# A two-layer hybrid transformer in one kernel: four steps of lead at the ends of a phase, later transposes, paired attention scores

## The chip, the cores and the metric

The kernel runs on one core of one Trainium2 chip. The metric is the device time of one execution in microseconds. Within a core five engines work side by side, each on its own queue in order: PE (matrix multiply; its weight loads are listed apart, as PEld), DVE (vector), ACT (scalar functions), POOL, and SP, which here only issues DMAs.

## The reference

Two layers on 256 tokens of width 1024, everything in float32. A layer adds to the residual `x` a feed-forward block, a mixer and a second feed-forward block:

```python
x = x + 0.5 * swiglu(rms_norm(x, ffa_norm), ffa_w_in, ffa_w_out)     # 1024 -> 2*2816 -> 1024
h = rms_norm(x, mix_norm)
(c_q, c_kv, k_rope, g_q, g_k, g_v, g_b, g_a, g_z, m_qkv, gate_logits) = split(h @ w_in)
o_mla  = causal softmax attention, 8 heads, q and k of 96 made from c_q, c_kv and k_rope
o_gdn  = gated delta rule, 4 heads of 128, after a causal convolution over 4 tokens
o_moba = causal softmax attention, 8 heads of 64 (256 tokens are one block)
x = x + sum_n(sigmoid(gate_n) * (o_n @ w_branch_n)) @ w_out
x = x + 0.5 * swiglu(rms_norm(x, ffb_norm), ffb_w_in, ffb_w_out)
```

The delta rule needs the inverse of a unit lower triangular matrix for each head and chunk.

## The kernel before

**Weights.** A weight matrix is read in pieces of 128 x 1024 numbers (a Step). `fetch` (L238) issues the DMA of a piece into one of five `raw` buffers, and splits it in two halves, each by an ACT cast to the rounded part `wh` (L260) and a DVE subtraction for the rest `wl` (L261). There are seven `wh`/`wl` pairs (NW). A product is three matmuls: high by high, high by low, low by high (L280 to L282 with tokens as the stationary operand; L309/L311, L340 to L342 and L965/L966 with the weights as the stationary operand).

**Phases, steps and events.** Each layer has three phases: feed-forward, mixer, feed-forward. A plain step is used twice, once for each half of the tokens: t=0 (the first 128) and t=1. `phase` (L1185) lists these uses, the events: t=0 of a step runs SKEW = 3 steps ahead of t=1 throughout the phase, so a phase begins with three t=0 events and ends with three t=1 events. A joint step (both halves of the tokens at once) is used at its t=1 place. Each event has 6 to 12 matmuls, and after it `fetch` splits at most one more half, up to LEAD = 3 steps past the last t=0 step.

**Generators and ticks.** What follows a product (norms, transposes, softmax, the delta rule) is written as Python generators. `tick` (L133) runs after each event and resumes those that are due; `yield n` means n ticks later. `until` runs ticks without events until something that is needed has been emitted.

**The planner.** Outside the first few instructions the framework orders each engine's instructions by itself: of those that its own estimates hold ready, the one emitted first. So a `yield` moves the place of an instruction in that order and promises nothing.

**Three chains that end in transposes on PE.** `epi_first` (L466): ACT copies a product of the first feed-forward step (L471), one tick later PE transposes it (L476). `epi_kv` (L1027): keys of the first attention, the last DVE product is L1041, one tick later `qk_T` transposes (L997). `epi_m(1)` (L1087): keys of the third branch; POOL makes 1/norm (L364, L365), DVE multiplies (L1108), one tick later `qk_T` transposes (L997).

**Phase ends.** `residual` (L428) adds the last product to `x`, squares it on ACT, POOL takes the power -1/2 (L392), DVE scales (L396), and LAG = 2 ticks later PE transposes the result (L370) for the next phase. This happens for t=0 and three events later for t=1.

**Attention** (`attention`, L560; used for both softmax branches). A written list says in which order groups of heads get their scores (`s0`: the first 128 queries of four heads; `s1`: the other 128 of two heads) and pairs of heads their outputs (`o`). `scores` holds one of two PSUM banks (`hold`, L118), does the score matmuls of its heads one after the other (L574), adds the mask (L576), takes the maximum on DVE (L581), one tick later the exponentials on ACT (L586, bank free after that), one tick later the division (L592). `outputs` transposes (L604 to L606), copies on ACT (L608) and, a tick later, does two matmuls for each of two heads (L613, L614), the two heads on different column halves of the array. Entries of the list are Y_ATT = 3 ticks apart. In the first branch the heads have 96 rows; in the third they have 64, even heads on partitions 0 to 63 and odd heads on 64 to 127, and each `s0` or `s1` group there has heads of one parity only. Every float32 matmul here is two MATMUL instructions.

**Inverse** (`invert` in `gdn`, L739). For two levels, a product of 128 columns for each of 4 heads (L772), an ACT copy (L774), a second product of 128 columns (L780), and a DVE addition that takes only every second group of columns (L783). A `back` transpose (L669) begins each level; the first waits for a DMA that brings the diagonal blocks' inverses.

**Where a branch waits.** The first `w_branch` step of a branch calls `until` on that branch's output.

Of the kernel before, what the change touches and what calls it, by code (L numbers as in the profile page):

```python
# [12 lines left out]
OP = mybir.AluOpType  # L13
# [20 lines left out]

LEAD, SKEW = 3, 3
NB4, NB2, NRAW, NW = 15, 20, 5, 7
# [45 lines left out]
class Kern:  # L82
# [34 lines left out]

    def hold(self):  # L118

        while self.held["pm"] >= BANKS - 4:  # L120
            yield 1
        self.held["pm"] += 1

# [325 lines left out]
    def ffn(self, l, name, norm_after):  # L449
# [16 lines left out]
        def epi_first(t, ps):  # L466

            if t == 0:
                SG["first"] = self.b4().rearrange("p (k c) -> p k c", k=4)
            y = self.b2()  # L470
            nc.scalar.copy(y, ps)  # L471
            self.done("acc")
            yield 1
            p = self.tp()
            for k in range(4):
                nc.tensor.transpose(p[:, k * 128:(k + 1) * 128], y[:, k * 128:(k + 1) * 128], self.ident)  # L476
            g = SG["first"]
# [82 lines left out]
    def attention(self, plan, getq, getk, getv, rq, oT):  # L560
# [7 lines left out]

        def scores(hs, n, w, q0, dst):
            t = q0 // 128  # L570
            yield from self.hold()
            ps = self.pm().rearrange("p (h k) -> p h k", h=n)
            for i, h in enumerate(hs):
                mm(ps[:, i, :], getq(h)[:, q0:q0 + 128], getk(h)[:, 0:w], start=(i == 0), stop=False,  # L574
                   skip_group_check=True)
            mm(ps[:, :, w - 128:w], self.identb, self.maskA[:, None, :].to_broadcast([128, n, 128]), start=False, stop=True,  # L576
               skip_group_check=True)
            dh = hs[1] - hs[0]
            rqs = rq[t][:, hs[0]:hs[-1] + 1:dh]
            mx, nb, sm, rs = (self.sm(4)[:, 0:n] for _ in range(4))  # L580
            nc.vector.tensor_reduce(mx, ps, axis=AX.X, op=OP.max)  # L581
            nc.vector.scalar_tensor_tensor(nb, mx, -1.0, rqs, op0=OP.mult, op1=OP.mult)
            yield 1
            P = self.b2().rearrange("p (h k) -> p h k", h=n)
            for h in range(n):
                nc.scalar.activation(P[:, h, :], ps[:, h, :], AF.Exp, scale=rqs[:, h:h + 1], bias=nb[:, h:h + 1],  # L586
                                     accum_out=sm[:, h:h + 1])
            self.done("pm")
            yield 1
            nc.vector.reciprocal(rs, sm)  # L590
            for h in range(n):
                nc.scalar.activation(P[:, h, :], P[:, h, :], AF.Copy, scale=rs[:, h:h + 1])  # L592
            for i, h in enumerate(hs):
                dst[h] = P[:, i, :]
            left[0] -= 1

        def outputs(hs):
            while not all(h in P0 and h in P1 for h in hs):
                yield 1
            yield 1  # L600
            PT = []
            for h in hs:
                pt = self.tp().rearrange("p (j k) -> p j k", j=4)
                nc.tensor.transpose(pt[:, 0, :], P0[h], self.ident)  # L604
                nc.tensor.transpose(pt[:, 1, :], P1[h][:, 0:128], self.ident)
                nc.tensor.transpose(pt[:, 2, :], P1[h][:, 128:256], self.ident)  # L606
# [4 lines left out]
            for i, h in enumerate(hs):  # L611
# [7 lines left out]
        for what, hs in plan:  # L619
            if what == "o":  # L620
                yield from outputs(hs)
            else:
# [5 lines left out]
    def gdn(self, ready, sil, beta, g, zs, oT):  # L628
# [110 lines left out]
        def invert(c):  # L739
# [29 lines left out]
            for l in range(LEVELS - 1):  # L769
                p = v4(self.pm())  # L770
                for h in range(H):
                    mm(p[:, h, :], cm[:, h, :], zz[:, h, 0, :], start=True, stop=True)  # L772
                t1 = v4(self.b2())
                nc.scalar.copy(t1, p)  # L774
                cm = v4(self.b2())
                nc.gpsimd.tensor_tensor(cm, nk, brow(self.lev[l + 1]), op=OP.mult)
                yield Y_INV
                p = v4(self.pm())
                for h in range(H):
                    mm(p[:, h, :], zz[:, h, 1, :], t1[:, h, :], start=True, stop=True)  # L780
                even = lambda z: z.rearrange("p h (m s b) -> p h m s b", s=2, b=16 << l)[:, :, :, 0, :]
                v = even(zz[:, :, 0, :])
                nc.vector.tensor_tensor(v, even(p), v, op=OP.add)  # L783
                yield Y_INV
# [97 lines left out]
    def mixer(self, l, norm_after):  # L882
# [144 lines left out]
        def epi_kv(t, hg, ps):  # L1027
            p = ps.rearrange("p (h d) -> p h d", h=4)
            if ("av", t) not in d:
# [12 lines left out]
                                    rk[:, :, None].to_broadcast([128, 4, 32]), op=OP.mult)  # L1042
            yield 1
            qk_T(t, y, 96, ("akT", hg))
# [15 lines left out]
        def attend():  # L1060
# [11 lines left out]
            while not all(("turned", ("mT", i), 1) in d for i in range(2)) or ("mv", 1) not in d:  # L1072
# [14 lines left out]
        def epi_m(i):  # L1087
            def f(t, ps):
# [16 lines left out]
                else:  # L1105
                    self.rsq(r, r, EPS, 1.0 / 64)
                    yield 2
                    nc.vector.tensor_tensor(y, y, r[:, :, None].to_broadcast([128, 8, 64]), op=OP.mult)  # L1108
                    yield 1
                qk_T(t, y.rearrange("p (k j) d -> p k (j d)", j=2), 128, ("mT", i))  # L1110
# [72 lines left out]


    def phase(self, steps, nacc):  # L1185

        n = len(steps)
        self.nacc = nacc
        ev = [(0, i) for i in range(SKEW)]
        for i in range(SKEW, n):  # L1190
            ev += [(1, i - SKEW), (0, i)]
        ev += [(1, i) for i in range(n - SKEW, n)]
        for t, i in ev:
# [4 lines left out]
            if t == 0:  # L1198
# [3 lines left out]
                if s.before:  # L1202
                    s.before()
            self.fetch(self.splits < 2 * (self.head + 1 + LEAD))
            if s.joint:
                for _ in s.use(s.wh, s.wl):
                    self.tick()
                    self.fetch(self.splits < 2 * (self.head + 1 + LEAD))
            else:
                s.use(t, s.wh, s.wl)  # L1210
            self.tick()
            if t == 1:
                s.wh = s.wl = s.raw = None
        self.base += n

    def run(self):
        self.setup()
        self.ss = {}
        self.base = self.loaded = self.splits = self.head = 0
        gains = [(n, l) for l in range(L) for n in ("ffa_norm", "mix_norm", "ffb_norm")]  # L1220
# [77 lines left out]
```

## Time and profile before

| what | value |
|---|---|
| three runs | 1353.65, 1350.1, 1348.01 us; median 1350.1 us |
| the profiled execution's own time | 1350.52 us |
| its span, first to last instruction | 1348.5 us |
| PE busy | 1320.3 us, 98% of the span |
| DVE, ACT, POOL busy | 937.4, 786.9, 117.9 us (70%, 58%, 9%) |
| granted PE clock, mean | 1.000 |
| HBM | 227.11 MB read, 170 GB/s over the span |

Busy time of PE is the time in which at least one matmul is under way, from its start to its modelled end; neighbouring matmuls overlap, so the distance from one start to the next is what a matmul costs in a full stream. An idle time stands in square brackets with the instruction that ended it.

### The profile page before, as it was taken

Reading aid. Unit: us, or ns where it says so; the run is one execution under the profiler, and the core shown is the slowest. Engines: PE = TensorE matmul, PEld = TensorE weight load, DVE = VectorE, ACT = ScalarE, POOL = GpSimd, SP = SyncE. Lnnn points to the kernel's source line nnn. Section 1 sums busy time; section 2 is a strip of 40 time slices with the busy share of each in tenths; the row PEclk is TensorE's granted clock in tenths of the full one; section 3 lists DMA queues with packets and bytes.
Section 4 is the critical chain, followed back from the end, with each engine's and each line's share of the span. In section 5 each row is a group of like instructions: output and inputs, shape, how many; then the busy total and the mean of one; then the engine's idle time right before and its main releaser. Section 6 shows DMA issues by size and latency. Waiting matters only on the chain.

```text
span 1348.5 us, 21398 instructions
## 1 busy us (share of the span) xinstructions
PE 1320.3 (98%) x7786; PEld 1150.3 (85%) x7786; DVE 937.4 (70%) x1890; ACT 786.9 (58%) x1783; POOL 117.9 (9%) x157
## 2 busy tenths in 40 slices
PE   6999999999999999999999999999999999999998
PEld 5888888788999988888888888887889999888887
DVE  6777558888457677775577775588865576777752
ACT  6666447776654556664466654487656544666642
POOL 0010003711101000000000000044120000000000
PEclk9999999999999999999999999999999999999999
DMA  8765566566343657665666556555553445666551
GB/s 277 233 221 185 177 181 167 145 169 176 103 131 110 188 156 218 188 189 176 197 196 194 185 176 184 158 173 160 153 157 99 139 127 171 187 188 189 191 184 62
DMA packets 207561, 231.25 MB, mean 171 GB/s; under 512 B 15616, under 2 KB 166112, under 8 KB 207456
## 3 DMA queue, kind: packets, MB, share of 16 engines
q1 hardware_dynamic: 207456, 229.89, 56.4%
q8 instruction: 61, 1.00, 0.3%
q14 instruction: 44, 0.36, 0.1%
HBM read 227.11 MB, written 2.75 MB: 170 GB/s over the span
## 4 chain that ended last, share of the span: by engine, by line
PE 92%; DVE 3%; ACT 2%; POOL 1%; DMA 1%; issue 1%; SPq 0%; DVEq 0%; ACTq 0%; POOLq 0%
PE acc L309 22%; PE acc L311 11%; PE acc L280 10%; PE acc L282 10%; PE acc L281 10%; PE acc L340 5%; PE acc L341 5%; PE acc L342 5%; PE acc L965 3%; PE pm L574 2%; PE acc L966 1%; ACT wh L260 1%; DMA raw<-in_ffa_w_in 1%; DVE wl L261 1%; PE tp L370 1%; PE pm L613 1%
## 5 line engine op out<-in xcount | busy, mean ns | idle before, releaser
L261 DVE TENSOR_TENSOR wl<-raw,wh 128x512 fp32r<-128x512 f32 (+1 forms) x844 | 563.2, 687 | 265.7 <-ACT wh L260 265.4
L260 ACT CAST wh<-raw 128x512 fp32r<-128x512 f32 (+1 forms) x844 | 497.2, 619 | 389.7 <-issue 147.4
L309 PE MATMUL acc<-q,wh 128*128 128x512 f32 x1280 | 449.3, 396 | 0.0
L311 PE MATMUL acc<-q,wl 128*128 128x256 f32 x1280 | 359.2, 281 | 0.0
L309 PEld LDWEIGHTS acc<-q,wh 128*128 128x128 f32 x1280 | 240.1, 188 | 55.8
L280 PE MATMUL acc<-wh,q 128*128 128x512 f32 (+2 forms) x656 | 259.1, 395 | 1.4 <-ACT q L358 1.4
L282 PE MATMUL acc<-wh,q 128*128 128x512 f32 (+2 forms) x656 | 256.1, 390 | 0.0
L281 PE MATMUL acc<-wl,q 128*128 128x512 f32 (+2 forms) x656 | 255.5, 390 | 0.0
L311 PEld LDWEIGHTS acc<-q,wl 128*128 128x128 f32 x1280 | 242.4, 189 | 0.5
L340 PE MATMUL acc<-q,wh 128*128 128x256 f32 x576 | 168.3, 292 | 0.0
L341 PE MATMUL acc<-q,wh 128*128 128x256 f32 x576 | 163.2, 283 | 0.4 <-DVE q L359 0.4
L342 PE MATMUL acc<-q,wl 128*128 128x256 f32 x576 | 163.0, 283 | 0.0
L280 PEld LDWEIGHTS acc<-wh,q 128*128 128x128 f32 x656 | 123.9, 189 | 26.3 <-ACT q L358 2.4
L282 PEld LDWEIGHTS acc<-wh,q 128*128 128x128 f32 x656 | 123.5, 188 | 26.2 <-DVE q L359 2.2
L281 PEld LDWEIGHTS acc<-wl,q 128*128 128x128 f32 x656 | 123.8, 189 | 21.7
L340 PEld LDWEIGHTS acc<-q,wh 128*128 128x128 f32 x576 | 110.3, 192 | 1.8 <-issue 1.0
L341 PEld LDWEIGHTS acc<-q,wh 128*128 128x128 f32 x576 | 110.3, 191 | 1.2 <-DVE q L359 0.8
L342 PEld LDWEIGHTS acc<-q,wl 128*128 128x128 f32 x576 | 110.1, 191 | 0.1
L965 PE MATMUL acc<-q,wh 128*128 128x512 f32 x192 | 70.5, 406 | 0.0
L486 DVE TENSOR_TENSOR d<-d,acc 128x256 f32<-128x256 f32 x160 | 66.5, 416 | 5.3 <-ACT d L484 5.3
L484 ACT COPY d<-acc 128x256 f32<-128x256 f32 x160 | 58.8, 368 | 18.9 <-PE acc L311 18.8
L392 POOL TENSOR_TENSOR s<-s,mhalf 128x1 f32<-128x1 f32 x12 | 8.3, 691 | 634.3 <-DVE s L385 634.3
(203 smaller groups left out, 1280.9 us busy)
## 6 DMA issues: line engine op xcount, KB each, us to landing
raw<-in_w_in SPq DMA_DIRECT2D x104, 512.0 KB
raw<-in_ffa_w_in SPq DMA_DIRECT2D x88, 512.0 KB
raw<-in_ffb_w_in SPq DMA_DIRECT2D x88, 512.0 KB
raw<-in_ffa_w_out SPq DMA_DIRECT2D x44, 512.0 KB
raw<-in_ffb_w_out SPq DMA_DIRECT2D x44, 512.0 KB
raw<-in_w_branch SPq DMA_DIRECT2D x24, 512.0 KB
raw<-in_w_out SPq DMA_DIRECT2D x16, 512.0 KB
raw<-in_w_in SPq DMA_DIRECT2D x8, 416.0 KB
```

Of the source, the lines that this page charges most:

```text
L260: nc.scalar.copy(s.wh[:, v], s.raw[:, v])
L261: nc.vector.tensor_sub(s.wl[:, v], s.raw[:, v], s.wh[:, v].bitcast(F32))
L280: mm(o, xh, wh[:, j, :], start=(k == 0), stop=False)
L281: mm(o, xh, wl[:, j, :], start=False, stop=False)
L282: mm(o, xl, wh[:, j, :], start=False, stop=(k == nk - 1))
L309: mm(ps.rearrange("p (s c) -> p s c", s=2), wh[:, k, v], x2, start=(g == 0 and k == 0), stop=False, skip_group_check=True)
L311: mm(ps[:, 0:256], wl[:, k, v], x2[:, 0, :], start=False, stop=last, skip_group_check=True)
L340: mm(o, wh[:, k, v], xh, start=(g == 0 and c == 0 and k == 0), stop=False, skip_group_check=True)
L341: mm(o, wh[:, k, v], xl, start=False, stop=False, skip_group_check=True)
L342: mm(o, wl[:, k, v], xh, start=False, stop=(4 * g + k == nk - 1), skip_group_check=True)
L486: nc.vector.tensor_tensor(dst, dst, ps[:, 0:256], op=OP.add)
L965: mm(p, wh[:, k, :], self.X[k // 2][:, k % 2], start=(k == 0), stop=False, skip_group_check=True)
```

## The change

It has five parts, in one diff. (1) t=0 runs four steps ahead (WIDE) at the start and at the end of each phase and three elsewhere; `ahead` keeps the splits within the seven buffers. (2) `epi_first`, `epi_kv` and `epi_m(1)` transpose one tick later. (3) `scores` takes a list of groups, holds as many banks, and issues their matmuls in turn; the list of the third branch now pairs an even group with an odd one (7 entries for 10). (4) `outputs` issues the larger matmuls of both heads, then the smaller ones. (5) the two products of the inverse are done on the 64 columns a head that are used.

```diff
-LEAD, SKEW = 3, 3
+LEAD, SKEW, WIDE = 3, 3, 4
-    def hold(self):
-        while self.held["pm"] >= BANKS - 4:
+    def hold(self, n=1):
+        while self.held["pm"] + n > BANKS - 4:
             yield 1
-        self.held["pm"] += 1
+        self.held["pm"] += n
...
             y = self.b2()                      # epi_first
             nc.scalar.copy(y, ps)
             self.done("acc")
-            yield 1
+            yield 2
...
-        def scores(hs, n, w, q0, dst):
+        def scores(groups, n, w, q0, dst):
...
-            for i, h in enumerate(hs):
-                mm(ps[:, i, :], getq(h)[:, q0:q0 + 128], getk(h)[:, 0:w], start=(i == 0), stop=False,
-                   skip_group_check=True)
-            mm(ps[:, :, w - 128:w], self.identb, self.maskA[:, None, :].to_broadcast([128, n, 128]), start=False, stop=True,
-               skip_group_check=True)
+            yield from self.hold(len(groups))
+            banks = [self.pm().rearrange("p (h k) -> p h k", h=n) for _ in groups]
+            for i in range(n):
+                for hs, ps in zip(groups, banks):
+                    mm(ps[:, i, :], getq(hs[i])[:, q0:q0 + 128], getk(hs[i])[:, 0:w], start=(i == 0), stop=False,
+                       skip_group_check=True)
+            for ps in banks:
+                mm(ps[:, :, w - 128:w], self.identb, self.maskA[:, None, :].to_broadcast([128, n, 128]), start=False,
+                   stop=True, skip_group_check=True)
...
-            for i, h in enumerate(hs):
-                ov = o[64 * i:64 * i + 64, :]
-                mm(ov, getv(0, h), PT[i][:, 0:256], start=True, stop=False, skip_group_check=True)
-                mm(ov[:, 128:256], getv(1, h), PT[i][:, 256:384], start=False, stop=True, skip_group_check=True)
+            halves = [(o[64 * i:64 * i + 64, :], h, PT[i]) for i, h in enumerate(hs)]
+            for ov, h, pt in halves:
+                mm(ov, getv(0, h), pt[:, 0:256], start=True, stop=False, skip_group_check=True)
+            for ov, h, pt in halves:
+                mm(ov[:, 128:256], getv(1, h), pt[:, 256:384], start=False, stop=True, skip_group_check=True)
...
             for l in range(LEVELS - 1):        # invert
-                p = v4(self.pm())
+                even = lambda z: z.rearrange("p h (m s b) -> p h m s b", s=2, b=16 << l)[:, :, :, 0, :]
+                half = lambda z: z[:, 0:256].rearrange("p (h c) -> p h c", h=H)
+                v = even(zz[:, :, 0, :])
+                p = half(self.pm())
                 for h in range(H):
-                    mm(p[:, h, :], cm[:, h, :], zz[:, h, 0, :], start=True, stop=True)
-                t1 = v4(self.b2())
+                    mm(p[:, h, :], cm[:, h, :], v[:, h], start=True, stop=True)
+                t1 = half(self.b2())
...
-                nc.vector.tensor_tensor(v, even(p), v, op=OP.add)
+                nc.vector.tensor_tensor(v, p.rearrange("p h (m b) -> p h m b", b=16 << l), v, op=OP.add)
...
-                [("s0", (0, 2, 4, 6)), ("s0", (1, 3, 5, 7)), ("s1", (0, 2)), ("s1", (1, 3)), ("o", (0, 1)),
-                 ("s1", (4, 6)), ("o", (2, 3)), ("s1", (5, 7)), ("o", (4, 5)), ("o", (6, 7))],
+                [("s0", (0, 2, 4, 6), (1, 3, 5, 7)), ("s1", (0, 2), (1, 3)), ("o", (0, 1)), ("s1", (4, 6), (5, 7)),
+                 ("o", (2, 3)), ("o", (4, 5)), ("o", (6, 7))],
...
+    def ahead(self):
+        return self.splits < 2 * min(self.head + 1 + LEAD, self.tail + NW)
...
-        ev = [(0, i) for i in range(SKEW)]
-        for i in range(SKEW, n):
-            ev += [(1, i - SKEW), (0, i)]
-        ev += [(1, i) for i in range(n - SKEW, n)]
+        ev = [(0, i) for i in range(WIDE)]
+        a, b = WIDE, 0
+        while b < n:
+            ev.append((1, b))
+            b += 1
+            while a < n and a - b < (WIDE if b < 2 or a > n - 4 else SKEW):
+                ev.append((0, a))
+                a += 1
...
-            self.fetch(self.splits < 2 * (self.head + 1 + LEAD))
+            self.fetch(self.ahead())
```

In `epi_kv` and `epi_m(1)` the last `yield 1` ahead of `qk_T` is a `yield 2`, as in `epi_first`; `self.tail` is the number of steps whose t=1 use is done.

## Rows read from the trace of the kernel before

**Rows 1.** The page, part 1: busy us, share of the span and count by engine.
```profile
PE 1320.3 (98%) x7786; PEld 1150.3 (85%) x7786; DVE 937.4 (70%) x1890; ACT 786.9 (58%) x1783; POOL 117.9 (9%) x157
```

**Rows 2.** Waits of PE: total us, times, longest us.
```profile
PE tp L370 <- DVE d L396: 12.0, 8, 9.3
PE tp L669 <- DMA q<-zd: 4.5, 4, 1.4
PE tp L997 <- DVE d L1108: 4.2, 4, 1.4
```

**Rows 3.** Timeline near 255 us: start, duration, engine, line, operation, idle before.
```profile
254.60 0.40 PE L965 MATMUL acc<-q,wh 128*128 128x512 f32 x1
...
255.72 0.63 PE L997 MATMUL tp<-ident,d 128*128 128x128 f32 x4 [0.72 <-DVE d L1108]
```

**Rows 4.** Timeline near 262 us, the same chain for t=1.
```profile
260.94 1.78 POOL L365 TENSOR_TENSOR s<-s,mhalf 128x8 f32<-128x8 f32 x1
...
261.75 0.48 PE L282 MATMUL acc<-wh,q 128*128 128x512 f32 x1
...
262.76 0.73 DVE L1108 TENSOR_TENSOR d<-d,s 128x512 f32<-128x512 f32 x1 [1.53 <-POOL s L365]
...
263.64 0.63 PE L997 MATMUL tp<-ident,d 128*128 128x128 f32 x4 [1.41 <-DVE d L1108]
```

**Rows 5.** Timeline near 29 us, the transposes of epi_first for t=1.
```profile
28.44 0.28 PE L311 MATMUL acc<-q,wl 128*128 128x256 f32 x1
...
28.80 0.28 PE L311 MATMUL acc<-q,wl 128*128 128x256 f32 x1
...
29.51 0.66 PE L476 MATMUL tp<-ident,d 128*128 128x128 f32 x4 [0.44 <-ACT d L471]
```

**Rows 6.** Timeline of PE around one s0 group of the third branch.
```profile
340.22 0.28 PE L342 MATMUL acc<-q,wl 128*128 128x256 f32 x1
340.43 1.16 PE L574 MATMUL pm<-q,q 64*128 64x128 f32 x8
...
341.55 0.47 PE L340 MATMUL acc<-q,wh 128*128 128x256 f32 x1
341.86 0.28 PE L341 MATMUL acc<-q,wh 128*128 128x256 f32 x1
```

**Rows 7.** Timeline of PE around one s1 group of the third branch.
```profile
356.06 0.28 PE L342 MATMUL acc<-q,wl 128*128 128x256 f32 x1
356.27 1.13 PE L574 MATMUL pm<-q,q 64*128 64x256 f32 x4
...
357.37 0.36 PE L340 MATMUL acc<-q,wh 128*128 128x256 f32 x1
357.57 0.28 PE L341 MATMUL acc<-q,wh 128*128 128x256 f32 x1
```

**Rows 8.** Timeline of PE in two output groups, of 291 and 303 us.
```profile
291.08 0.66 PE L613 MATMUL pm<-d,d 128*64 128x256 f32 x4
291.56 0.40 PE L614 MATMUL pm<-d,d 128*64 128x128 f32 x4
...
303.08 0.81 PE L613 MATMUL pm<-d,d 128*64 128x256 f32 x3
...
303.94 0.38 PE L614 MATMUL pm<-d,d 128*64 128x128 f32 x2
```

**Rows 9.** Timeline of PE: one column against 128, both with 128-column weights.
```profile
319.15 1.59 PE L683 MATMUL tp<-cst,q 128*128 128x1 f32 x13
...
338.02 1.05 PE L772 MATMUL pm<-q,d 128*128 128x128 f32 x8
```

**Rows 10.** Costliest groups by line (count, busy us, mean ns): ACT's softmax.
```profile
L586 ACT ACTIVATE d<-pm,s,s 128x128 f32<-128x128 f32 (+1 forms) x64 | 32.0, 508 | 18.9 <-DVE s L582 18.9
...
L592 ACT ACTIVATE d<-d,s 128x128 f32<-128x128 f32 (+1 forms) x64 | 25.2, 457 | 1.7 <-DVE s L590 1.6
```

**Rows 11.** Waits of ACT for a weight buffer that PE still reads.
```profile
ACT wh L260 <- PE acc L341: 70.1, 44, 4.1
```

More of the change, by code (lines that the diff above doesn't have):

```diff
@@ L567, in attention @@
         left = [len(plan)]
-        def scores(hs, n, w, q0, dst):
+        def scores(groups, n, w, q0, dst):
             t = q0 // 128
-            yield from self.hold()
-            ps = self.pm().rearrange("p (h k) -> p h k", h=n)
-            for i, h in enumerate(hs):
-                mm(ps[:, i, :], getq(h)[:, q0:q0 + 128], getk(h)[:, 0:w], start=(i == 0), stop=False,
-                   skip_group_check=True)
-            mm(ps[:, :, w - 128:w], self.identb, self.maskA[:, None, :].to_broadcast([128, n, 128]), start=False, stop=True,
-               skip_group_check=True)
[L578 to L582, printed above, removed]
-            yield 1
[L584 to L588, printed above, removed]
-            yield 1
-            nc.vector.reciprocal(rs, sm)
-            for h in range(n):
-                nc.scalar.activation(P[:, h, :], P[:, h, :], AF.Copy, scale=rs[:, h:h + 1])
-            for i, h in enumerate(hs):
-                dst[h] = P[:, i, :]
@@ new lines, in scores @@
+            made = []
+            for hs, ps in zip(groups, banks):
+                rqs = rq[t][:, hs[0]:hs[-1] + 1:hs[1] - hs[0]]
+                mx, nb = (self.sm(4)[:, 0:n] for _ in range(2))
+                nc.vector.tensor_reduce(mx, ps, axis=AX.X, op=OP.max)
+                nc.vector.scalar_tensor_tensor(nb, mx, -1.0, rqs, op0=OP.mult, op1=OP.mult)
+                made.append((hs, ps, rqs, nb))
+            yield 1
+            soft = []
+            for hs, ps, rqs, nb in made:
+                P, sm = self.b2().rearrange("p (h k) -> p h k", h=n), self.sm(4)[:, 0:n]
+                for h in range(n):
+                    nc.scalar.activation(P[:, h, :], ps[:, h, :], AF.Exp, scale=rqs[:, h:h + 1], bias=nb[:, h:h + 1],
+                                         accum_out=sm[:, h:h + 1])
+                self.done("pm")
+                soft.append((hs, P, sm))
@@ L595, in scores @@
+            yield 1
+            for hs, P, sm in soft:
+                rs = self.sm(4)[:, 0:n]
+                nc.vector.reciprocal(rs, sm)
+                for h in range(n):
+                    nc.scalar.activation(P[:, h, :], P[:, h, :], AF.Copy, scale=rs[:, h:h + 1])
+                for i, h in enumerate(hs):
+                    dst[h] = P[:, i, :]
             left[0] -= 1
@@ L610, in outputs @@
             o = self.pm()[:, 0:256]
-            for i, h in enumerate(hs):
-                ov = o[64 * i:64 * i + 64, :]
-                mm(ov, getv(0, h), PT[i][:, 0:256], start=True, stop=False, skip_group_check=True)
-                mm(ov[:, 128:256], getv(1, h), PT[i][:, 256:384], start=False, stop=True, skip_group_check=True)
+            halves = [(o[64 * i:64 * i + 64, :], h, PT[i]) for i, h in enumerate(hs)]
[3 more added lines that the diff above has]
+                mm(ov[:, 128:256], getv(1, h), pt[:, 256:384], start=False, stop=True, skip_group_check=True)
             k = hs[0] // 2
@@ L617, in outputs @@
             left[0] -= 1
-        for what, hs in plan:
+        for what, *hs in plan:
             if what == "o":
-                yield from outputs(hs)
+                yield from outputs(hs[0])
             else:
@@ L777, in invert @@
                 yield Y_INV
-                p = v4(self.pm())
+                p = half(self.pm())
                 for h in range(H):
                     mm(p[:, h, :], zz[:, h, 1, :], t1[:, h, :], start=True, stop=True)
-                even = lambda z: z.rearrange("p h (m s b) -> p h m s b", s=2, b=16 << l)[:, :, :, 0, :]
-                v = even(zz[:, :, 0, :])
-                nc.vector.tensor_tensor(v, even(p), v, op=OP.add)
+                nc.vector.tensor_tensor(v, p.rearrange("p h (m b) -> p h m b", b=16 << l), v, op=OP.add)
                 yield Y_INV
@@ L1042, in epi_kv @@
                                     rk[:, :, None].to_broadcast([128, 4, 32]), op=OP.mult)
-            yield 1
+            yield 2
             qk_T(t, y, 96, ("akT", hg))
@@ L1108, in f @@
                     nc.vector.tensor_tensor(y, y, r[:, :, None].to_broadcast([128, 8, 64]), op=OP.mult)
-                    yield 1
+                    yield 2
                 qk_T(t, y.rearrange("p (k j) d -> p k (j d)", j=2), 128, ("mT", i))
@@ L1207, in phase @@
                     self.tick()
-                    self.fetch(self.splits < 2 * (self.head + 1 + LEAD))
+                    self.fetch(self.ahead())
             else:
@@ L1213, in phase @@
                 s.wh = s.wl = s.raw = None
+                self.tail = g + 1
         self.base += n
@@ L1218, in run @@
         self.ss = {}
-        self.base = self.loaded = self.splits = self.head = 0
+        self.base = self.loaded = self.splits = self.head = self.tail = 0
         gains = [(n, l) for l in range(L) for n in ("ffa_norm", "mix_norm", "ffb_norm")]
```

## The prediction

> **What bounds the kernel now.** I read the page first: PE is busy for 1320.3 of 1348.5 us, and no other engine is above 70% [rows 1]. So PE is the bound, and the change can win in two ways only: where PE idles (28.2 us by that row), or where its matmuls take longer than they must. Busy time hides the second. I therefore read PE's waits next and then the distances between the starts of neighbouring matmuls, in the timeline. Of the idle time, 12.0 us stand at the transposes after a norm, but 9.3 of them are one wait, the start of the kernel; seven at phase ends share 2.7. The other two large ones are 4.5 us for the DMA ahead of the inverse and 4.2 us at L997 for DVE's L1108 [rows 2].
>
> **The later transposes (part 2).** Before L997 a 512-column matmul starts at 254.60 and the transposes only at 255.72 [rows 3]; such a matmul takes 0.24 of a stream (the pair of 512 and 256 columns takes 28.80 - 28.44 = 0.36, its larger part two thirds) [rows 5], so 0.88 is lost. For t=1 it is 263.64 - 261.75 - 0.24 = 1.65; there L1108 itself came late, because POOL's power of 1.78 us ended just before it [rows 4]. Both waits are for L1108, and recur in layer two: four times, 4.2 us by the waits view [rows 2], 2 x (0.88 + 1.65) = 5.06 by the starts. One tick more puts one event between: four pairs of 0.36 [rows 5], 1.44 us. That covers 0.88 whole and leaves 0.21 of the 1.65: gain 2 x (0.88 + 1.44) = 4.6. L1108 itself isn't moved, so nothing on DVE or POOL changes. Bounds: 0, if the planner puts the transposes where they were, and 5.06. In `epi_first` the transposes start 0.71 after a 256-column matmul that takes 0.12 [rows 5]: 0.6 gained, once. `epi_kv` had no wait: 0. But its keys are now a tick later, so the first attention starts and ends a tick later, and the first `w_branch` step, which by the code's order already spends two ticks without events waiting for it, spends three. The tick more holds a product of the inverse (eight matmuls of L772) that only changes places with the step behind it: 0; were it a bare wait, it would be one event, 1.44 a layer.
>
> **Scores in turn (part 3).** An s0 group now costs: the matmul before it starts at 340.22 and would be done after 0.12; the next stream starts at 341.55 and its second matmul 0.31 later instead of 0.12: 1.33 - 0.12 + 0.19 = 1.40 [rows 6]. An s1 group: 357.37 - 356.06 - 0.12 + 0.08 = 1.27 [rows 7]. Six groups a layer, two s0 and four s1, become three pairs. In a pair, the even heads sit on partitions 0 to 63 and the odd ones on 64 to 127, so two halves of the array work. No row shows two row halves at work together; the nearest is the output groups, where two heads use the two column halves: four L613 and four L614 take 291.08 to 291.56 + 0.40 = 0.88, tail included, while one head's four alone would stream 2 x 0.24 + 2 x 0.12 = 0.72 [rows 5, 8]. Two heads thus cost hardly more than one. If row halves do the same, the second group of a pair costs only its mask, 0.2 for s0 and 0.1 for s1: 1.40 - 0.2 = 1.2 and 1.27 - 0.1 = 1.17 saved, a layer 1.2 + 2 x 1.17 = 3.5, both layers 7.1. The other end: the halves take turns, and a pair saves only the gaps on either side of a group: 340.43 - 340.22 - 0.12 = 0.09 before, and about the same twice after (first to second matmul, last to mask), 0.28 x 6 = 1.7. I take 6.5, near the upper end, because the output row is that near.
>
> The Trainium skill, TensorE: Matmul & The Clock Gate, section "Part 3: Packing small matmuls", gives 3.07 times for four row tiles, 77% of the ideal. No run here shows it; as an estimate from that page a pair would stream 0.86 / 0.77 instead of 0.86 and the gain of this part would be 7.1 - 6 x 0.26 = 5.5.
>
> Softmax comes in bursts of two groups. ACT needs (32.0 + 25.2) / 24 groups = 2.4 us a group [rows 10], 4.8 a pair, and two pairs are three ticks apart, 4.3 us: ACT falls behind by one or two us beside its splits. In this stretch the steps are joint, so their halves are split six steps, twelve events, ahead of use: 17 us of cover. I count 0.5 against the change for banks that come free later; between 0 and the rival below.
>
> **Outputs (part 4).** In program order L614 of the first head stands before L613 of the second. In the first group of [rows 8] all four L613 start before any L614, so PE already pulls the second head forward, and the new order gains nothing; only the group of 303 us, where the second head's copy was late, runs 303.08 to 303.94 + 0.38 = 1.24 instead of 0.88. It and its like in layer two: 2 x 0.36 = 0.7 at most, I take 0.6.
>
> The same section of the Trainium skill has matmuls start and end strictly in program order. By that rule sixteen output groups would each have waited as the slow one did, and the reorder would be worth 16 x 0.36 = 5.8. The trace disagrees for the group of 291 us, and the measurement decides.
>
> **The inverse (part 5).** 64 MATMULs each at L772 and L780 go from 128 to 64 columns. But 13 matmuls of one column take 1.59 and 8 of 128 columns 1.05: five more for 0.54, 0.11 each [rows 9], the same price whatever the columns, since both load 128 columns of weights. So 0 on PE. The upper end, half price, is 128 x 0.054 = 6.9. ACT's shorter copies are off the path.
>
> **Four steps ahead (part 1).** The transposes after a norm stay two ticks behind their product, and it is these two events that don't cover the chain; an event between them and the next phase covers what wasn't late. So the 2.7 [rows 2] stays: 0. It may win up to 2.7 where DVE is less crowded. At the kernel's start step 3 is wanted one event earlier, 1.44 at worst.
>
> **Sum.** 4.6 + 0.6 + 6.5 + 0.6 - 0.5 = 11.8 off the profiled execution's own 1350.5 us: 1338.7. The median of the runs, 1350.1, is 0.4 lower: 1338.3, said as 1338.5.
>
> **Rivals.**
> - Row halves take turns: 1.7 instead of 6.5, so 1343.3. For it: no row shows them together. Against: the column halves [rows 8].
> - The planner undoes the later transposes, or PE waits as long for something behind them: 4.6 goes, 1343.1. For it: L1108 waits for POOL, not for its place [rows 4]. Against: an event of ready matmuls stands between.
> - PE pays by columns in the inverse: 1338.5 - 6.9 = 1331.6. Against it: [rows 9].
> - Slower: at each edge of a phase four steps of lead and three of splits fill all seven weight buffers, so ACT's cast of the next step waits until PE has left the oldest one, and everything behind it on ACT, the norm's square among it, waits too. Such waits take 1.6 us each now (70.1 / 44) [rows 11]. If PE waits as long at both ends of six phases and the pairs don't run together, 12 x 1.6 = 19.2 against 7.0 of gains: 1362.3. It decides once a cast comes later than three steps of lead, 8.6 us, can hide; the waits now are at most 4.1.
>
> **Chances.** Forecast 0.57; turns 0.15; transposes undone 0.12; columns 0.06; slower 0.10 in all shades. The range 1332 to 1348 leaves out both ends' extremes, about 0.15; the likeliest case alone is 1335 to 1342. What this measurement can tell from no change is about 0.5%, 6.75 us: below 1343.4 counts as faster. Forecast and columns fall there nearly whole (0.61), the two near 1343 about half (0.13), so faster 0.74; the slower case counts beyond 1356.9 for 0.05; the rest, 0.21, is no change.
>
> **What would show it.** PE's wait for L1108 near 0.2 instead of 4.2 in all; the L574 groups of the third branch three a layer, eight or sixteen matmuls with starts in pairs about 0.01 apart and a length like one group's now; L772 still 1.05 for eight; PE idle at phase ends unchanged. Wrong would be paired starts spaced as single ones, a new row of PE waiting for ACT between 340 and 400 us, or for a cast at a phase's beginning.

## The result, and the profile after

The changed kernel takes 1338.82 us in the median (1338.29 to 1339.80), beside 1351.88 for the kernel before on the same chip: a ratio of 0.9906 (95% interval 0.9889 to 0.9923). The forecast was 1338.5. The total came out. Of the larger terms behind it only the pairs of scores did; the others are errors that happen to cancel, so the closeness of the total is luck.

The page of the changed kernel, part 1, beside [rows 1]: PE is busy 7.4 us less in a span that is 12.3 us shorter, so idle time went as well as stream time.

```profile
span 1336.2 us, 21427 instructions
PE 1312.9 (98%) x7786; PEld 1144.8 (86%) x7786; DVE 939.3 (70%) x1890; ACT 784.6 (59%) x1783; POOL 119.7 (9%) x157
```

Waits of PE in the changed kernel (total us, times, longest), beside [rows 2]. Line numbers are larger than before: L370 is L371 here, L669 is L681, L997 is L1011, L1041 is L1055, L1108 is L1122.

```profile
PE tp L371 <- DVE d L397: 13.1, 11, 8.8
PE tp L1011 <- DVE d L1055: 2.2, 4, 0.8
...
PE acc L342 <- DVE q L360: 1.1, 1, 1.1
PE tp L681 <- DMA q<-zd: 0.8, 1, 0.8
PE tp L1011 <- DVE d L1122: 0.5, 2, 0.3
```

Three readings. The wait for the key product of the third branch (now L1122) fell from 4.2 to 0.5, but a new one of 2.2 stands beside it, for the keys of `epi_kv` (L1055). The wait for the DMA of the inverse, in which nothing was expected to change, fell from 4.5 to 0.8. And the waits after a norm, without the start of the kernel, rose from seven of 2.7 to ten of 13.1 - 8.8 = 4.3.

The answer to [rows 3, 4]: POOL, DVE and PE of the changed kernel near 260 us (start, duration, engine, line, operation, idle before).

```profile
258.62 1.03 POOL L366 TENSOR_TENSOR s<-s,mhalf 128x4 f32<-128x4 f32 x1
...
259.68 0.42 DVE L1053 TENSOR_TENSOR d<-pm,s 128x256 f32<-128x256 f32 x1 [1.00 <-POOL s L366]
...
260.02 1.78 POOL L366 TENSOR_TENSOR s<-s,mhalf 128x8 f32<-128x8 f32 x1
260.02 0.28 DVE L1055 TENSOR_TENSOR d<-kr,s 128x128 f32<-128x128 f32 x1
260.45 0.61 PE L1011 MATMUL tp<-ident,d 128*96 128x128 f32 x4 [0.77 <-DVE d L1055]
261.83 0.73 DVE L1122 TENSOR_TENSOR d<-d,s 128x512 f32<-128x512 f32 x1 [1.53 <-POOL s L366]
262.71 0.52 PE L1011 MATMUL tp<-ident,d 128*128 128x128 f32 x3 [0.25 <-DVE d L1122]
```

DVE waits twice for POOL's power, 1.00 and 1.53, once for each chain, and the powers stand one behind the other: 258.62 to 259.65, then 260.02 to 261.80. Before, PE stopped at the second; now it stops at the first, and the second is nearly covered.

The answer to [rows 6, 7]: a pair of s0 groups and a pair of s1 groups.

```profile
337.78 1.16 PE L577 MATMUL pm<-q,q 64*128 64x128 f32 x16
...
339.13 0.47 PE L341 MATMUL acc<-q,wh 128*128 128x256 f32 x1
...
345.88 1.13 PE L577 MATMUL pm<-q,q 64*128 64x256 f32 x8
...
347.10 0.36 PE L341 MATMUL acc<-q,wh 128*128 128x256 f32 x1
```

Sixteen MATMULs take 1.16 us, as eight did before, and eight take 1.13, as four did; by the single records the two halves start 0.006 to 0.007 apart.

The answer to [rows 8, 9]: the output group that was slow, and the inverse's product.

```profile
302.45 0.65 PE L624 MATMUL pm<-d,d 128*64 128x256 f32 x2 [0.23 <-ACT d L619]
...
304.75 0.38 PE L626 MATMUL pm<-d,d 128*64 128x128 f32 x2
...
330.51 1.00 PE L788 MATMUL pm<-q,d 128*128 128x64 f32 x8
```

The slow group stayed slow: its first head starts at 302.45, PE does matmuls of another step between, and the second head is not done before 304.75 + 0.38. Eight products of 64 columns take 1.00 where 128 columns took 1.05; by the distances between starts, up to the matmul that follows, such a group costs 0.87 us in both. For [rows 5], the transposes of `epi_first` follow their neighbour with no wait:

```profile
29.69 0.28 PE L312 MATMUL acc<-q,wl 128*128 128x256 f32 x1
29.81 0.60 PE L477 MATMUL tp<-ident,d 128*128 128x128 f32 x4
```

For [rows 10, 11], ACT's exponentials in the groups by line (count, busy us, mean ns), and ACT's waits for a weight buffer in the whole execution, which did not get longer:

```profile
L594 ACT ACTIVATE d<-pm,s,s 128x128 f32<-128x128 f32 (+1 forms) x64 | 32.0, 516 | 16.6 <-DVE s L587 14.5 <-PE tp L617 2.2
```

```profile
ACT wh L261 <- PE acc L342: 55.9, 38, 3.7
```

### The profile page after: what moved, and what is told of

Same layout as the page of the kernel before. It is cut to its first block, busy times and chain, and to the rows that moved or that the text cites. A ratio compares the mean times of both kernels' runs of the same rounds, so it can differ in the third digit from the quotient of the medians.

```text
span 1336.2 us, 21427 instructions
## 1 busy us (share of the span) xinstructions
PE 1312.9 (98%) x7786; PEld 1144.8 (86%) x7786; DVE 939.3 (70%) x1890; ACT 784.6 (59%) x1783; POOL 119.7 (9%) x157
## 4 chain that ended last, share of the span: by engine, by line
PE 91%; POOL 3%; DVE 2%; ACT 2%; issue 1%; DMA 1%; SPq 0%; POOLq 0%; DVEq 0%; ACTq 0%
PE acc L310 22%; PE acc L312 11%; PE acc L281 10%; PE acc L283 10%; PE acc L282 10%; PE acc L341 5%; PE acc L342 5%; PE acc L343 5%; PE acc L979 3%; PE acc L980 1%; PE pm L577 1%; POOL s L366 1%; PE tp L371 1%; ACT wh L261 1%; PE pm L624 1%
## 5 line engine op out<-in xcount | busy, mean ns | idle before, releaser
L310 PE MATMUL acc<-q,wh 128*128 128x512 f32 x1280 | 448.3, 394 | 0.0
L310 PEld LDWEIGHTS acc<-q,wh 128*128 128x128 f32 x1280 | 239.8, 187 | 55.2
L281 PE MATMUL acc<-wh,q 128*128 128x512 f32 (+2 forms) x656 | 257.9, 393 | 1.4 <-ACT q L359 1.4
L341 PE MATMUL acc<-q,wh 128*128 128x256 f32 x576 | 167.8, 291 | 0.0
L281 PEld LDWEIGHTS acc<-wh,q 128*128 128x128 f32 x656 | 123.7, 189 | 26.3 <-ACT q L359 2.4
L341 PEld LDWEIGHTS acc<-q,wh 128*128 128x128 f32 x576 | 109.9, 191 | 2.3 <-issue 1.0
```

Source lines behind the costliest of these rows:

```text
L281: mm(o, xh, wh[:, j, :], start=(k == 0), stop=False)
L310: mm(ps.rearrange("p (s c) -> p s c", s=2), wh[:, k, v], x2, start=(g == 0 and k == 0), stop=False, skip_group_check=True)
L341: mm(o, wh[:, k, v], xh, start=(g == 0 and c == 0 and k == 0), stop=False, skip_group_check=True)
```

## The experiments

All ratios are to the kernel before, with their 95% interval. 0.001 is 1.35 us. One caution holds for all of them: the 1280 matmuls of the FFN at L309 (L310 after), which no edit touches, streamed at a pace that differs between executions, at a granted clock of 1.00 or just under in each. By the distances between their starts they took 299.2 us in the profile of before, 298.0 in that of the change, and up to 302.9 in others. So differences of less than some 3 us between medians are not relied on here (an estimate from that spread), and where two variants of the change are compared, PE's waits and the other lines decide.

**Part 2 alone.** Three chains one tick later, on the kernel before.

```diff
 epi_first, epi_kv, epi_m(1), ahead of the transposes:
-            yield 1
+            yield 2
```

> Part 2 alone: the kernel before, with the three chains' transposes one tick later. Theory A (the wait only changes its name: the transposes of t=1 still stand 0.4 to 1.0 us behind their 512-column matmul, and the keys of epi_kv become a new wait for L1041): 0.7 + 0.6 = 1.3 us gained, PE's waits for L1041 about 2.2 us, and the DMA wait ahead of the inverse (4.5) and the solve wait (1.7) unchanged. Theory B (the tick more also moves the attention's last events and so removes the DMA wait): as A, and PE's wait for q<-zd at L669 falls from 4.5 to about 0.8: 5.0 us gained. The prediction's own step says 5.2 us gained without a change at L669.

Measured: 0.9956 (0.9944 to 0.9967), 5.9 us faster. Waits of PE in this run:

```profile
PE tp L997 <- DVE d L1041: 2.3, 4, 0.8
PE acc L341 <- DVE q L359: 1.7, 2, 1.0
...
PE pm L821 <- ACT d L837: 1.4, 2, 0.7
PE tp L997 <- DVE d L1108: 0.8, 4, 0.2
...
PE tp L669 <- DMA q<-zd: 0.2, 1, 0.2
```

Theory B: the transposes themselves gain 4.2 - 0.8 - 2.3 = 1.1, and the DMA wait gives 4.5 - 0.2 = 4.3. The first product of `w_branch` (L341) waits 1.7 for the branch's output where it waited 0.4. With L476's 0.4 that sums to 1.1 + 4.3 + 0.4 - 1.3 = 4.5, and the two profiled executions differ by 1350.5 - 1346.1 = 4.4. Two terms that this sum leaves out cancel: the first matmul came 0.8 earlier, and the outputs' stream grew by 0.8 (see "The outputs back"). The solve wait (L821, 1.4 in the kernel before too) is not part 2's.

**Part 3 alone.** Scores in turn and the list of seven entries.

```diff
-                [("s0", (0, 2, 4, 6)), ("s0", (1, 3, 5, 7)), ...
+                [("s0", (0, 2, 4, 6), (1, 3, 5, 7)), ("s1", (0, 2), (1, 3)), ...
```

> Part 3 alone: the kernel before, with the scores of two groups in turn in the third branch, and its list of seven entries. Theory A (the gain is the pairs themselves, two row halves at work together): 6.4 us gained, the three pairs of a layer with starts about 0.01 apart, the DMA wait ahead of the inverse 4.5 us as before, the solve wait (L821 behind L835, 0.86 a layer) as before. Theory B (the shorter list also takes the solve wait away): 6.4 + 1.7 = 8.1. The prediction's step says 6.0.

Measured: 0.9933 (0.9920 to 0.9946), 9.1 us faster. Waits of PE:

```profile
PE tp L679 <- DMA q<-zd: 5.4, 4, 1.4
PE tp L1007 <- DVE d L1118: 4.2, 4, 1.4
```

The wait for L1118 (L1108 before) stays as it was, the DMA wait is 0.9 longer, and there is no row for the solve's product any more. Theory B: pairs and solve wait.

**Part 1 alone.** Four steps ahead at a phase's ends.

```diff
+            while a < n and a - b < (WIDE if b < 2 or a > n - 4 else SKEW):
+                ev.append((0, a))
```

> Part 1 alone: the kernel before, with four steps of lead at a phase's ends. Theory A (the lead costs at the phase ends: transposes after a norm wait longer behind the splits): about 2 us slower at the phase ends, waits at L370 13.1 instead of 12.0 and more, DMA wait at L669 as before. Theory B (the lead's other rule for splits takes work off DVE in the mixer's middle, so the small solve chain ends some 3 us earlier and the DMA wait ahead of the inverse falls by 3.7): about 2 to 4 us faster in sum. The prediction's step says 0.

Measured: 1.0022 (1.0012 to 1.0031), 3.0 us slower, just at the limit named above. Waits of PE:

```profile
PE tp L371 <- DVE d L397: 13.4, 11, 9.2
PE tp L670 <- DMA q<-zd: 5.8, 4, 1.9
```

Theory A at the phase ends; the DMA wait, which it left as it was, grew by 1.3. Of the three waits more at L371, the timeline of the changed kernel shows one, for t=1 at the end of the second phase:

```profile
484.53 0.66 PE L371 MATMUL tp<-ident,d 128*128 128x128 f32 x4 [0.59 <-DVE d L397]
...
491.62 0.39 PE L283 MATMUL acc<-wh,q 128*128 128x512 f32 x1
492.40 0.63 PE L371 MATMUL tp<-ident,d 128*128 128x128 f32 x4 [0.40 <-DVE d L397]
```

The kernel before had the first of the two (493.63, 0.53) and not the second: there the transposes for t=1 started 0.23 after the matmul ahead of them. DVE is not later: from the start of `residual`'s addition to the start of the scaling it takes 3.07 us in the kernel before and 3.04 in the changed one, by the trace. PE is sooner: it starts 14 matmuls in that time and up to the transposes where it started 17, and stands at them 3.54 us after the addition's start instead of 4.07. The two other ends where a wait is new show the same. Without part 1 it is 17 again, and no wait.

**Part 5 alone.** The inverse on 64 columns.

```diff
-                    mm(p[:, h, :], cm[:, h, :], zz[:, h, 0, :], start=True, stop=True)
+                    mm(p[:, h, :], cm[:, h, :], v[:, h], start=True, stop=True)
```

> Part 5 alone: the kernel before, with the inverse's products on 64 columns instead of 128. The prediction's step and theory A: the eight matmuls of L772 and L780 cost 1.00 instead of 1.05, 0.65 us gained at most. Theory B (ACT's and DVE's shorter copies also remove the solve wait of 0.86 a layer): 2.4 us gained. Rival of the prediction (PE pays by columns): 6.9 gained.

Measured: 1.0008 (1.0000 to 1.0016). No gain; the prediction's 0. The solve wait was there (1.4).

**The keys back.** The changed kernel, `epi_kv` at one tick.

```diff
 epi_kv:
-            yield 2
+            yield 1
             qk_T(t, y, 96, ("akT", hg))
```

> The changed kernel, with the transposes of epi_kv back at one tick; the other two chains stay one tick later. Theory A (of part 2, the keys' tick is the one that moves the third branch, the solve chain or its reading behind, and so removes the DMA wait): PE's wait for L1055 (2.2 us) goes, but the DMA wait for q<-zd comes back from 0.8 to about 4.5: 1.5 us slower than the changed kernel. Theory B (the tick in epi_m does it, because the transposes of the key product no longer hold up what stands behind them): L1055's wait goes and the DMA wait stays below 1: 2.2 us faster than the changed kernel, a ratio of about 0.989 to the kernel before.

Measured: 0.9946 (0.9931 to 0.9961). Waits of PE:

```profile
PE tp L681 <- DMA q<-zd: 5.4, 4, 1.5
PE tp L1011 <- DVE d L1055: 3.0, 4, 1.0
```

Theory A in its main point: of the three edits in part 2, the one costed at nothing removes the DMA wait. Wrong in the other: L1055's wait grows instead of going, so the keys' transposes wait even at their old place; that it is because those of L1122 no longer stop PE ahead of them is a reading of the rows, which no run isolates.

**The attention alone a tick later.** As the last, and the first attention starts one tick later.

```diff
 attend:
-            yield 1
+            yield 2
             d["oT", 0] = ...
```

> The changed kernel with the keys' transposes of epi_kv back at one tick (as in the run with the keys back, which had the DMA wait of 5.4 us again), and instead the first attention itself started one tick later. Theory A (it is the attention that must go a tick later: its work on DVE then stands behind the small solve chain and not ahead of it, the chain's end moves from PE's 1671st matmul to its 1661st): the DMA wait falls to below 1 us, a ratio of about 0.991; the keys' wait for L1055 stays 3.0. Theory B (it is the keys' transposes on PE or their copies on ACT that must move): the DMA wait stays about 5.4, a ratio of 0.9946 or more.

Measured: 0.9920 (0.9906 to 0.9935). No row for the DMA any more:

```profile
PE tp L1011 <- DVE d L1055: 3.0, 4, 1.0
PE acc L342 <- DVE q L360: 2.1, 2, 1.1
```

Theory A. It is the attention's own start that counts. The small solve chain is 30 short operations on DVE, with casts and the attention's work between them in its queue. This is the end of that chain in the first layer, the DMAs that SP issues around it, and PE's transposes of the result, in the kernel before, where they waited 1.41 us at 333.29 and 0.89 at 335.70:

```profile
325.05 0.16 DVE L724 TENSOR_TENSOR d<-d,d 64x15 f32<-64x15 f32 x1
325.15 0.37 SPq L249 DMA_DIRECT2D raw<-in_w_branch  x1
325.61 3.38 SPq L732 DMA_DIRECT2D zd<-d  x8
329.83 0.61 SPq L735 DMA_DIRECT2D q<-zd  x1
...
333.29 0.63 PE L669 MATMUL tp<-ident,q 128*128 128x128 f32 x4 [1.41 <-DMA q<-zd]
```

and in the changed one:

```profile
321.78 0.16 DVE L736 TENSOR_TENSOR d<-d,d 64x15 f32<-64x15 f32 x1
322.00 2.89 SPq L744 DMA_DIRECT2D zd<-d  x8
325.05 0.61 SPq L747 DMA_DIRECT2D q<-zd  x1
325.71 0.62 SPq L250 DMA_DIRECT2D raw<-in_w_branch  x1
...
330.01 0.66 PE L681 MATMUL tp<-ident,q 128*128 128x128 f32 x4
```

PE reaches these transposes with its 1716th matmul in both. Counted in PE's matmuls, which takes out that PE itself is ahead, the chain begins behind the 1545th and ends behind the 1671st in the kernel before, behind the 1539th and the 1661st in the changed one, with 9 casts between its operations instead of 11. In every profile where the first attention starts at its old tick (before, parts 1, 3 and 5 alone, keys back) the chain ends behind the 1671st matmul and PE waits 4.1 to 5.8 us; in all seven where it starts one tick later, behind the 1661st, with 0.8 at most.

The chain's earlier end on DVE is one half of it: PE arrives at the transposes 8.1 us after that end instead of 331.88 - 325.21 = 6.7. The other half is SP's queue. Before, SP issues the read of a `w_branch` piece just ahead of the chain's eight writes, and the first read of the result (`q<-zd`) is issued 329.83 - 325.21 = 4.62 us after the chain's end. In the changed kernel that piece stands behind the first read, which is issued 325.05 - 321.94 = 3.11 after the chain's end. The two groups keep apart in both layers: 4.5 to 5.2 us in the five profiles that wait, 3.1 to 3.6 in the others. So 1.5 of what the first transposes gain in time is SP's, beside 1.4 of the chain's end; that the one piece causes the whole 1.5 was not tested.

**Pairs, one group after the other.** The changed kernel, the two loops exchanged.

```diff
-            for i in range(n):
-                for hs, ps in zip(groups, banks):
+            for hs, ps in zip(groups, banks):
+                for i in range(n):
                     mm(ps[:, i, :], ...
```

> The changed kernel, with the matmuls of a pair of score groups in the order of before: all of the even heads, then all of the odd ones; list, banks and softmax as in the change. Theory A (the two row halves work together only where neighbours in the order use different halves): a pair of s0 takes 1.7 instead of 0.89 us, one of s1 1.5 instead of 0.75; some 2 x (0.85 + 2 x 0.7) = 4.5 us slower than the changed kernel, and the starts no longer come in pairs. Theory B (PE starts the second group early, as it does with the column halves of the outputs): no difference, starts still in pairs.

Measured: 0.9925 (0.9909 to 0.9942). PE's timeline, one pair of each kind:

```profile
338.91 1.71 PE L577 MATMUL pm<-q,q 64*128 64x128 f32 x16
...
347.56 1.14 PE L577 MATMUL pm<-q,q 64*128 64x256 f32 x8
```

Between the theories. A pair of s1 loses nothing (1.14 against 1.13): PE starts the odd heads 0.014 us behind the even ones although four MATMULs of the even ones stand ahead of them as written. (The trace shows starts, not the program's order; that the planner kept the written order is inferred from the s0 pair, where it shows.) A pair of s0 loses 1.71 - 1.16 = 0.55: with eight ahead, the odd heads start only when four of those have started, and then run beside the other four. So the order written in the change is worth 2 x 0.55 = 1.1 us; the larger part comes from putting the two groups side by side at all. In this profile the FFN's matmuls took 302.9 us against 298.0, which alone is more than the rest of the distance between the medians.

**The long list.** The changed kernel with three empty entries in the list, so that it has ten again.

```diff
-                [("s0", ...), ("s1", ...), ("o", (0, 1)), ...
+                [("s0", ...), ("w",), ("s1", ...), ("w",), ("o", (0, 1)), ...
```

> The changed kernel, with three empty entries in the third branch's list, so that it has ten entries again and ends as many ticks later as before; the pairs stay. Theory A (the list's length put the two products of the recurrence, L849 and L835 now, apart in the order, and that took the solve wait of 0.86 a layer away): the solve wait comes back, 1.7 us slower than the changed kernel. Theory B (the pairs' fewer streams do it): no difference.

Measured: 0.9924 (0.9906 to 0.9941). PE had no wait at the solve's product, so theory A is out: the length of the list isn't it. Its span is 6.5 us longer than the changed kernel's, 4.9 of it in the FFN's L310. In the other 1.6 stand a longer wait for L360 at `w_branch` (2.1 instead of 1.1) and a longer one at L281 (2.0 instead of 1.4); the rest was not traced. Which of the pairs' effects takes the solve wait away stays open.

**Without part 1.** The changed kernel with three steps of lead everywhere.

```diff
-        ev = [(0, i) for i in range(WIDE)]
+        ev = [(0, i) for i in range(SKEW)]
```

> The changed kernel without part 1: three steps of lead everywhere, and the old rule for splits. Theory A (part 1 alone cost 0.2% on the kernel before, and costs the same in company: transposes after a norm wait longer, 0.56 to 0.75 us at a phase end where they waited some 0.4): 2 to 3 us faster than the changed kernel, a ratio of about 0.9885 to the kernel before. Theory B (it is paid back by the start of the kernel or by the mixer in company with the later transposes): within 1 us of the changed kernel.

Measured: 0.9904 (0.9887 to 0.9920): within 1 us of the change by the medians, as theory B has it, but medians can't tell that much. Waits of PE:

```profile
PE tp L370 <- DVE d L396: 11.6, 8, 8.8
...
PE acc L341 <- DVE q L359: 2.1, 2, 1.1
```

The phase ends win 4.3 - 2.8 = 1.5, the DMA's 0.8 goes too, and `w_branch` loses 1.0. Outside the FFN's L309 PE was 1.6 us ahead of the changed kernel, in the FFN 2.9 behind. By the rows it lies between the theories, nearer to A.

**The keys three ticks behind**, with and without part 1.

```diff
 epi_kv:
-            yield 2
+            yield 3
```

> The changed kernel with the transposes of epi_kv three ticks behind instead of two, and the attention with them. Theory A (one tick more covers the keys' wait, but the first branch's outputs end a tick later too, and the first product of w_branch, which already waits 1.1 us for L360, waits a tick longer in each layer): L1055's 2.2 us go, L342's wait for L360 grows by 1.44 a layer: 0.7 us slower than the changed kernel. Theory B (the planner finds other work for PE): 2.2 us faster than the changed kernel, a ratio of about 0.989.

> As the run with the keys three ticks behind, and without part 1 as well: the candidate for a kernel faster than the changed one. Theory A (part 1 costs 2.1 us at the phase ends, where the second transposes after a norm wait 0.56 each; what it gave elsewhere was a cast's wait at w_branch, 1.0): 1 us faster than the run with the keys three ticks behind. Theory B (no difference in company, as without the third tick): the same within 1 us.

Measured: 0.9924 (0.9907 to 0.9941) and 0.9905 (0.9889 to 0.9921). Waits of PE in the first:

```profile
PE tp L1011 <- DVE d L1055: 2.8, 4, 1.0
...
PE tp L681 <- DMA q<-zd: 1.1, 2, 0.6
```

Both theories fall for the third tick: the wait for L1055 does not go, it is 3.0, 2.2 and 2.8 us at one, two and three ticks. `w_branch` doesn't wait longer either. The chain ends behind the 1670th matmul again, nearly where it ended before the change, and yet the DMA costs only 1.1 and 1.2 in the two runs, none of it at the first transposes: SP issues the first read 3.1 us after the chain's end there, so SP's order does most of it in these two. Part 1's removal gave 1.9 us outside the FFN's L310, on theory A's side, and the medians differ by 2.9. None of these beats the changed kernel by more than the measurement tells.

**The outputs back.** The changed kernel with the output products head by head.

```diff
-            for ov, h, pt in halves:
-                mm(ov, getv(0, h), ...
-            for ov, h, pt in halves:
-                mm(ov[:, 128:256], getv(1, h), ...
+            for i, h in enumerate(hs):
+                mm(ov, getv(0, h), ...
+                mm(ov[:, 128:256], getv(1, h), ...
```

> The changed kernel with the output products in the order of before, head by head. The prediction's step: 0.6 us slower. Theory A (PE starts the second head's products early by itself, up to four matmuls ahead as the pairs in the old order showed, and the slow groups waited for a copy of ACT): within 0.3 us by the sums at L624 and L626. Theory B (strict program order): 16 groups by 0.36, 5.8 us slower.

Measured: 0.9917 (0.9902 to 0.9932). By the distances between starts the two lines take 8.7 + 5.8 = 14.5 us instead of 8.4 + 5.6 = 14.0: 0.5. That this is near the prediction's 0.6 is chance, for it is no gain against the kernel before, where they took 8.2 + 5.5: part 2 alone raised them to 8.7 + 5.8, and part 4 takes some 0.5 of that back. It is all in the slow group, one a layer: 1.17 us of PE's time before, 1.59 with part 2 alone and in this run, 1.37 in the change. The other 14 groups take 0.80 or 0.81 in each.

## Why the prediction was right in its total and wrong in its steps

**Scores in turn: right.** By the prediction's own measure (end of the matmul before, to the second one after), a pair of s0 costs 1.63 now against 2 x 1.40, one of s1 1.39 against 2 x 1.27: 2 x (1.17 + 2 x 1.15) = 6.9 us, 6.5 forecast. The rival that row halves take turns is out. The 0.5 counted against the change for banks that come free later does not show: no score matmul has a row among PE's waits. The Trainium skill (TensorE: Matmul & The Clock Gate, "Part 3: Packing small matmuls") has 3.07 times for four row tiles, 77% of the ideal; with two row halves no such loss shows here: 16 MATMULs take the 1.16 us of 8.

**The later transposes: the step that failed.** It said that one event of ready matmuls covers 0.88 and 1.44 of each layer's two waits, 4.6 us. The wait for L1108 did go, by 3.7, but 2.2 came back at L1055; net 1.5. A tick more can't cover it: the row shows two powers of POOL one behind the other, DVE waiting for each, and PE stopping at whichever chain it meets first. The rival "PE waits as long for something behind them" had this half right, its place wrong (the keys, not something behind). That POOL is the cause rests on the rows and on the third tick that did not help; a kernel with the power on another engine was not run.

**The cost of `epi_kv` at nothing: wrong, and it saved the sum.** "So the first attention starts and ends a tick later" was seen, and only what PE has to wait at its end was asked. What it clears was not: DVE's queue ahead of the solve chain, and with it SP's queue ahead of the chain's DMAs. The DMA wait was counted as unchanged and gave 4.5 - 0.8 = 3.7 us. The two runs on the attention's start show it. The wait at `w_branch`, 1.06 in one layer, is the "bare wait" that was taken as 0 and bounded by 1.44: 0.7 in all over the 0.4 of before.

**The solve wait: missed.** 1.4 us; part 3 alone removes it and parts 1, 2 and 5 alone don't.

**Four steps ahead at 0: wrong by 1.6 us** against the change. It was argued that the transposes stay two ticks behind their product, and the argument stopped there; but PE has fewer matmuls between the last addition and the transposes, 14 instead of 17 by the trace, so PE comes to the transposes 0.5 us sooner and waits for a chain on DVE that takes as long as it did. Alone the part makes the kernel 0.2% slower. The rival with weight buffers did not come: ACT's waits for them are no longer than before.

**Outputs 0.6: wrong against the kernel before.** The slow group was to fall from 1.24 to 0.88. It became slower, 2.68 from its first start to its last end, because part 2 moved it; the outputs cost 0.3 more than before, and 0.2 of wait for ACT. By the same section of the Trainium skill, matmuls start strictly in program order, and by that rule the run with the outputs back would have been 5.8 us slower. The trace disagrees: it was 0.5, and in the pairs one by one PE started matmuls of the other half ahead of four that stand before them as written.

**`epi_first` 0.6, inverse 0: right.** `epi_first` had 0.4 of wait by the view, and it is gone.

**The sum by what was measured:** pairs 6.9, L1122 and L1055 1.5, DMA 3.7, solve 1.4, L476 0.4, start of the kernel 0.5 (9.3 to 8.8), less 0.7 at `w_branch` and 1.6 at phase ends: 12.1, beside 12.2 between the profiled executions. Forecast: 11.8. That it closes so well is luck too: it leaves out the outputs (-0.5) and the FFN's L309 (299.2 - 298.0 = 1.2, its pace, no effect of the change), with which it would be 12.8. Nor need the 0.5 at the start be an effect: the first matmul starts anywhere from 8.1 to 9.3 us in the fourteen profiles.

## What to carry to other kernels

- A tick of delay on a side chain is not an edit on that chain alone: ask what it moves out of the way on the shared in-order queues (here DVE's, and SP's with the DMAs), and which chain with a DMA behind it gets through earlier. Here that was worth 3.7 us, and the wait it was aimed at gave 1.5.
- A wait put down to one chain can be a queue of several on a slow engine: before costing its removal, list everything that engine does in the two microseconds ahead, and ask which of its other customers PE meets next.
- Two half-height groups side by side on the array's two row halves cost one, 1.16 us for 16 MATMULs as for 8. Write them in turn: in the two kinds of pair tried here, PE found the partner by itself with four matmuls between and not with eight.
- A lead counted in ticks is not a lead in time: at the phase ends the transposes stayed two ticks behind their product, and PE still came to them 0.5 us sooner.

## What the runs showed of the hardware that was not expected

- The same 1280 matmuls of 512 columns, untouched by any edit, took by their starts from 297.6 to 302.9 us in the fourteen profiles, with the granted clock at 0.999 or 1.0 in each. On the page, where matmuls overlap, the mean of one is 396 ns before, 394 after, and 399 with the pairs one by one, whose row this is.

```profile
L310 PE MATMUL acc<-q,wh 128*128 128x512 f32 x1280 | 453.4, 399 | 0.0
```

- The reach with which PE starts a matmul of the other array half early looks like four matmuls: an s1 group, four, did not hold its partner up at all, an s0 group, eight, for its first four.
- Halving the columns of a product with 128 columns of weights saved nothing: eight of them cost 0.87 us at L772 and at L788, by the starts and up to the next matmul.
